# A two-layer mixer and expert block: all RWKV steps traced ahead of their outputs' norms, w_out's products between the last steps, h's rows made once, x1's affine map on VectorE

## The chip, the cores and the metric

The kernel runs on 1 core of one Trainium2 chip. A core has five engines that each work through a queue of their own in order: TensorE (PE in the profile; PEld is its loading of weights), VectorE (DVE), ScalarE (ACT), GpSimd (POOL) and SyncE (SP, which here only issues transfers). ACT and POOL issue transfers too. The metric is the device time of one execution in microseconds (us), and less is better.

## The reference, cut to what matters

Two layers over 768 tokens of 1024 numbers (256 of context, 512 of latent; the second layer keeps the latent alone after its mixer). All of it is float32.

```
p        = modulated norm of x, times w_in                     # input side
y        = [ rwkv(p) (256) | s5(p) (256) | attention(p) (512) ]
m        = (y @ w_out) * gate[s]           # s: context or latent
x1       = layer_norm(ALPHA * x + m, ln1_g, ln1_b)
h        = x1 * (1 + scale[s]) + shift[s]  # what the experts read
E, w     = two of 32 experts and their weights from h @ w_router
x2       = layer_norm(ALPHA * x1 + experts(h, E, w) * gate2[s], ln2_g, ln2_b)

rwkv:  per head a 64x64 state S, forwards and backwards over the tokens,
       S_t = S_{t-1} * w_t - (S_{t-1} kk_t) b_t^T + v_t k_t^T,   y_t = S_t r_t
       y   = (group_norm(y_f + y_b) * gn_w + gn_b + bonus) * gate(g)
```

## The kernel before, in words

The tokens lie in six tiles of 128: 0 and 1 are context, 2 to 5 latent. The kernel's functions write instructions in some order, a scheduler at build time puts them into the engines' queues by that order and by what each waits for, and the chip then runs every queue strictly in order.

**The scan.** `rwkv` runs the scan in chunks of 64 tokens: 12 steps forwards (`f`) and 12 backwards (`g`), side by side. `step(n, d)` loads the chunk's operands into `rec` (SP), corrects them by the state (L631 on PE, L633 on DVE), forms the new state (L640, L647, L653, and L656 on POOL). `output` (L672, L676 on PE, L682 on DVE) adds what this chunk yields to the tile's `y`, and is written one step late. The forward scan takes chunk 0 to 11, the backward scan 3 to 0 and then 11 to 4; so tiles 0 and 1 are complete after step 3, tiles 3 and 4 after step 9, tiles 2 and 5 after step 11.

**What follows a complete tile.** `outputs(n)` calls `finish` for a pair of tiles as soon as it is complete (the table `groups`, L721). `finish` is the group norm and the gate: DVE L695 to L714 in turn with POOL L699 to L711, then two transposes on PE (L59) and a copy to `yo`.

**mixing** is a generator that `rwkv` advances through `fill`, between its steps, so many yields a call as the third numbers of the table `FILL` say; attention and the modulation's products are advanced by the first two.

- `part(i)` multiplies the attention's and S5's 768 of the 1024 rows of `w_out` (L1582: 12 products of 128x128 by 128x512, of which the trace shows two rows each), adds ALPHA * x (L1589, L1590 on DVE), and stores the tile to `mixq`.
- `hrows(s)` makes, for context and for latent, `w2` (the first 256 rows of `w_out` times the gate, L1612 on POOL) and the two rows `hg`, `hb` of h's affine map, each spread over 128 partitions (L1615 to L1617, three POOL multiplications of 128x1024).
- `norm(i)` multiplies `yo` by `w2` (L1635 on PE), adds to `q` (the stored part), takes the statistics (L1641 to L1643 on DVE), a power on POOL (L86, L87), makes `h` by two 128x1024 operations on DVE (L1646, L1647), stores it to `hd`, and transposes it (L59; the copies to `hT` at L1656, one on DVE and one on ACT).
- `affine` makes x1 from `q`: L1659 on DVE, L1660 on ACT, L1661 and L1662 on POOL (128x1024 each), and a store that POOL issues. It is written after the next tile's norm has begun.
- `rt.logits` multiplies `hT` by the router (L1395, L1398, L1401); `rt.choose` is a chain of some 27 small DVE operations (L1423 to L1453) for two tiles, and the `rank` that it returns puts their tokens into the table of the experts' slots (PE L1458 to L1462, DVE L1464 to L1469, POOL's scatters L1473). `rt.finish` reads the table back; then tokens are gathered from `hd` (L1855), and `experts` begins with `xT` (L59 into `b_m`) and L1762.

The loop of `mixing` takes a pair of tiles through its norms once both are in `ys` and their parts are done, and otherwise makes one more part:

```python
        g = groups[0]
        if all(i in ys and i in ready for i in g):
            groups.pop(0)
            ...
            pend.insert(0, rt.choose([i - t0 for i in g]))
        else:
            if parts:
                ready.append(parts.pop(0))
                part(ready[-1])
```

`k.bank()` takes the next PSUM bank of the stream that is set; `k.free` names the streams that the last norms take instead.

After the mixer the experts' weights (3 tensors of 2 MB for each of 32 experts, from SP) stream in; the first two experts' before the first gather, the third's after it.

Of the kernel before, what the change touches and what calls it, by code (L numbers as in the profile page):

```python
# [324 lines left out]
def rwkv(k, l, st, cvd, Y, ys, streams, fill):  # L325
# [448 lines left out]
    fill('end')  # L774
# [772 lines left out]
def mixing(k, l, sO, sR, before, yd, ys, x_src, x1, hd, NTOK):  # L1547
# [8 lines left out]
    qd = k.dram('mixq%d' % l, [6, 128, D])  # L1556
    t0 = 6 - NTOK // 128
# [7 lines left out]
    gt = {}  # L1565

    def gate(s):
        if gt.get('s') != s:
            gt.update(s=s, t=brow(k, O, 'gt', mr[s, 0]))
        return gt['t']  # L1570

    def part(i):
# [13 lines left out]
        for h in range(2):  # L1586
            c = slice(512 * h, 512 * h + 512)
            o = O.tile([128, 512], F32, name='oq', bufs=2)
            V.tensor_tensor(o, ps[h], g[:, c], op=ALU.mult)  # L1589
            V.scalar_tensor_tensor(x[:, c], x[:, c], ALPHA, o, op0=ALU.mult, op1=ALU.add)  # L1590
# [3 lines left out]
    ready = []  # L1594
    for _ in range(2):
        ready.append(parts.pop(0))
        part(ready[-1])
        yield
    before()
# [7 lines left out]
    def hrows(s):  # L1607

        if rows.get('s') != s:
# [4 lines left out]
            t = P.tile([128, D], F32, name='h', bufs=2)  # L1614
# [51 lines left out]
    groups = [g for g in ((0, 1), (3, 4), (2, 5)) if g[0] >= t0]  # L1666
    pend = []

    while groups:
        g = groups[0]  # L1670
        if all(i in ys and i in ready for i in g):
            groups.pop(0)
            for j, i in enumerate(g):
                hT, late = norm(i)
                while pend:
                    pend.pop(0)()
                rt.logits(j, hT)
                (pend if groups else rt.late).append(late)
                if j == 0:
                    yield  # L1680
            pend.insert(0, rt.choose([i - t0 for i in g]))
            k.normed = not groups
            yield
        else:
            if parts:
                ready.append(parts.pop(0))
                part(ready[-1])
            while pend:
                pend.pop(0)()
            k.rest = not parts  # L1690
            yield
    while pend:
        pend.pop(0)()
# [334 lines left out]
FILL = ({'front': ((1, 0, 0), (1, 3, 0)), 'back': ((1, 3, 0),), 'inverse': ((4, 6, 0), (4, 4, 0)), 'step': ((3, 2, 0), (3, 3, 0), (2, 4, 0), (3, 3, 0), (3, 3, 0), (0, 2, 2), (0, 2, 0), (0, 0, 5))}, {'front': ((1, 0, 0), (1, 0, 0)), 'back': ((0, 0, 0), (1, 4, 0), (1, 2, 0), (1, 2, 0)), 'inverse': ((1, 9, 0),), 'step': ((2, 5, 0), (1, 4, 0), (2, 6, 0), (2, 3, 0), (1, 1, 0), (0, 0, 2), (1, 0, 0), (0, 0, 3))})  # L2028
# [56 lines left out]
def trunk(tc, a, out):  # L2085
    k = K(tc, a)
    nc = k.nc
    with ExitStack() as st:
# [50 lines left out]
        for l in range(2):  # L2139
# [45 lines left out]
            with ExitStack() as s1:  # L2185
# [4 lines left out]
                k.free = [('f', 2), ('g', 2)]  # L2190
# [79 lines left out]
```

## Time and profile before

| what | value |
|---|---|
| median of three runs | 2879.89 us (2876.12 to 2887.47) |
| the profiled execution | 2857.41 us |
| its span, first to last instruction | 2855.6 us |
| busy in the span: PE, DVE, POOL, ACT | 2201.2, 1185.0, 869.6, 524.8 us |
| TensorE clock granted, mean | 0.882 of full speed |
| moved by the transfers | 691.51 MB, 242 GB/s over the span |

The profiled execution is 22.5 us quicker than the median of the three. The stretch that the change touches is the end of each layer's scan and what lies between it and the experts: about 505 to 530 us (a place where an instruction is moved to) and 730 to 931 us in layer 0, 2130 to 2284 us in layer 1. Layer 0's experts run from 931 us, layer 1's from 2284 us.

### The profile page before, as it was taken

Reading aid. Unit: us, or ns where it says so; the run is one execution under the profiler, and the core shown is the slowest. Engines: PE = TensorE matmul, PEld = TensorE weight load, DVE = VectorE, ACT = ScalarE, POOL = GpSimd, SP = SyncE. Lnnn points to the kernel's source line nnn. Section 1 sums busy time; section 2 is a strip of 40 time slices with the busy share of each in tenths; the row PEclk is TensorE's granted clock in tenths of the full one; section 3 lists DMA queues with packets and bytes.
Section 4 is the critical chain, followed back from the end, with each engine's and each line's share of the span. In section 5 each row is a group of like instructions: output and inputs, shape, how many; then the busy total and the mean of one; then the engine's idle time right before and its main releaser. Section 6 shows DMA issues by size and latency. Waiting matters only on the chain. (4 is left out here: it accounts for less than half of the span.)

```text
span 2855.6 us, 43442 instructions
## 1 busy us (share of the span) xinstructions
PE 2201.2 (77%) x16189; PEld 1472.1 (52%) x16189; DVE 1185.0 (41%) x2830; ACT 524.8 (18%) x1264; POOL 869.6 (30%) x1189
## 2 busy tenths in 40 slices
PE   5898677878683888889874788787797397888882
PEld 3787455666442544555544676556554254454441
DVE  7972556563556000010006883666546611111114
ACT  2222333222001100011005222343120100000001
POOL 2651543331345111101105662544334510111002
PEclk8999788698886999999996899698799699999996
DMA  8334667665536899998875224556784799988994
GB/s 243 93 94 113 167 189 195 160 174 179 164 122 237 331 416 371 392 381 353 358 280 206 69 73 125 145 147 173 214 232 136 243 375 417 417 357 351 383 420 190
DMA packets 411611, 691.51 MB, mean 242 GB/s; under 512 B 146178, under 2 KB 315906, under 8 KB 394912
## 3 DMA queue, kind: packets, MB, share of 16 engines
q1 hardware_dynamic: 310368, 594.85, 58.2%
q10 hardware_dynamic: 72640, 58.03, 6.9%
q0 software_dynamic: 28288, 34.32, 3.7%
q8 instruction: 211, 3.46, 0.5%
q14 instruction: 104, 0.85, 0.1%
HBM read 607.98 MB, written 95.44 MB: 246 GB/s over the span
## 5 line engine op out<-in xcount | busy, mean ns | idle before, releaser
L1762 PE MATMUL b_m<-w,xT 128*64 128x256 f32 x4928 | 593.1, 396 | 129.3 <-DMA w<-in_expert_w_gate_dram 76.7
L1762 PEld LDWEIGHTS b_m<-w,xT 128*64 128x64 f32 x4928 | 391.6, 142 | 333.5 <-issue 150.4
L243 PE MATMUL b_m<-xT,win 128*128 128x256 f32 (+1 forms) x1416 | 276.2, 355 | 8.5 <-POOL xT L167 3.7
L243 PEld LDWEIGHTS b_m<-xT,win 128*128 128x128 f32 x1416 | 232.7, 201 | 42.9 <-POOL xT L167 4.5
L1786 PE MATMUL b_m<-w,aT 128*64 128x512 f32 x1024 | 231.0, 592 | 1.1 <-issue 0.6
L1775 DVE COPY aT<-b_m 128x256 f32<-128x256 f32 x64 | 27.2, 425 | 473.6 <-PE b_m L59 473.6
L1792 POOL DMA_INDIRECT yb<-y,dx x64 | 63.8, 997 | 427.0 <-DVEq L1907 257.3
L1786 PEld LDWEIGHTS b_m<-w,aT 128*64 128x64 f32 x1024 | 76.4, 137 | 117.1 <-issue 108.1
L1764 ACT ACTIVATE act<-b_m 128x256 f32<-128x256 f32 x64 | 24.5, 383 | 568.6 <-PE b_m L1762 556.9
L877 PE MATMUL b_a<-kz,qb 128*128 128x128 f32 (+2 forms) x416 | 113.2, 415 | 15.7 <-ACT pr L898 10.0
L1765 DVE TENSOR_TENSOR act<-act,b_m 128x256 f32<-128x256 f32 x64 | 27.0, 421 | 234.2 <-PE b_m L1762 234.2
L1582 PE MATMUL b_a<-wo,yt 128*128 128x512 f32 x240 | 111.6, 614 | 0.0
L1792 POOL DMA_INDIRECT yb<-yo,dx x13 | 12.9, 994 | 290.0 <-ACTq L1907 146.6
L877 PEld LDWEIGHTS b_a<-kz,qb 128*128 128x128 f32 x416 | 76.9, 232 | 40.5 <-ACT pr L898 11.8
L127 PE MATMUL b_a<-wmod,cc 128*32 128x128 f32 x1280 | 69.4, 329 | 35.1 <-DMA wmod<-in_w_mod_dram 29.1
L59 PE MATMUL b_a<-idf,pr 128*128 128x128 f32 x320 | 56.5, 299 | 29.6 <-DVE pt L921 11.0
L1855 POOL DMA_INDIRECT xg<-hd,ix x32 | 33.2, 1037 | 141.7 <-PE b_m L59 126.9
L1582 PEld LDWEIGHTS b_a<-wo,yt 128*128 128x128 f32 x240 | 44.9, 194 | 50.9 <-issue 49.7
L127 PEld LDWEIGHTS b_a<-wmod,cc 128*32 128x32 f32 x1280 | 40.9, 126 | 55.1 <-DMA wmod<-in_w_mod_dram 22.2
L551 POOL TENSOR_TENSOR tl<-Bm,Xh 112x4 f32<-112x4 f32 (+13 forms) x112 | 39.7, 354 | 92.5 <-DVE Xh L552 48.5
L1791 DVE TENSOR_TENSOR y<-b_m,gate 128x512 f32<-128x512 f32 x32 | 22.1, 692 | 95.0 <-PE b_m L1786 95.0
L656 POOL TENSOR_TENSOR sn<-st,gc 128x128 f32<-128x128 f32 x44 | 23.2, 529 | 121.4 <-DVE st L647 117.1
(542 smaller groups left out, 4061.5 us busy)
## 6 DMA issues: line engine op xcount, KB each, us to landing
w<-in_expert_w_gate_dram SPq DMA_DIRECT2D x64, 2048.0 KB
w<-in_expert_w_up_dram SPq DMA_DIRECT2D x64, 2048.0 KB
w<-in_expert_w_down_dram SPq DMA_DIRECT2D x64, 2048.0 KB
wmod<-in_w_mod_dram SPq DMA_DIRECT2D x80, 512.0 KB
rec<-rec SPq DMA_DIRECT2D x40, 512.0 KB
win<-in_w_in_dram SPq DMA_DIRECT2D x16, 1024.0 KB
wmod<-in_w_mod_dram SPq DMA_DIRECT2D x4, 2048.0 KB
sca<-sc SPq DMA_DIRECT2D x24, 256.0 KB
```

The costliest lines, as they stand in the source:

```text
L59: k.nc.tensor.transpose(out, x, k.idf[r:r + n, r:r + n])
L127: nc.tensor.matmul(p[32 * g:32 * g + 32, :], k.cc[:, kk, :], wt[:, kk, :], start=kk < 4, stop=kk >= 4, tile_position=(0, 32 * g))
L243: nc.tensor.matmul(p[:, :n], wt[u][:, kk, j * 128:j * 128 + 128], xT[v][:, kk, c0:c0 + n], start=kk == 0 and q == 0, stop=kk == 7 and q == 2)
L551: eng.tensor_tensor(t[:, 0:n, j:32], Bm[:, r0:r1, j:j + 1].to_broadcast([112, n, w]), x.to_broadcast([112, n, w]), op=ALU.mult)
L877: nc.tensor.matmul(dst, qb[:, 2 * v + e, :], kz[:, v, r, 128 * keys[c][0]:128 * keys[f - 1][0] + 128], start=c == 0 or (c == 4 and r == 0) ...
L1582: nc.tensor.matmul(ps[h], y[:, kt, :], wo[:, kt, 512 * h:512 * h + 512], start=kt == 0, stop=kt == 5)
L1762: mm = nc.tensor.matmul(p[64 * h:64 * h + 64, 0:256], xT[:, kk, :], w[:, kk, 256 * h:256 * h + 256], start=kk == 0, stop=kk == 7)
L1765: nc.vector.tensor_tensor(a, a, pu[:, 0:256], op=ALU.mult)
L1775: k.nc.vector.tensor_copy(aT, pa[:, 0:256].rearrange("p (j x) -> p j x", j=2))
L1786: nc.tensor.matmul(py[64 * s:64 * s + 64, :], aT[:, j, 64 * h:64 * h + 64], wd[:, q, 512 * s:512 * s + 512], start=q == 0, stop=q == 3)
L1792: sc = nc.gpsimd.indirect_dma_start(out=yb, out_offset=bass.IndirectOffsetOnAxis(ap=dst, axis=0), in_=y, in_offset=None, bounds_check=3071 ...
L1855: return nc.gpsimd.indirect_dma_start(out=out, out_offset=None, in_=hd, in_offset=bass.IndirectOffsetOnAxis(ap=idx, axis=0), bounds_check= ...
```

## The change

`finish` is called for tiles 0 and 1 after step 3 in layer 0 as before; for the pairs (3, 4) and (2, 5) it is written after all steps. `mixing` makes all parts first and then all norms in one written order, and `FILL` gives the last steps fewer yields each (2, 2, 2, 1 where each had 5 in layer 0; 1, 1, 0 where each had 3 in layer 1). `gated(s, pool)` makes `w2` from the row `gt` that `part` has loaded, and is written earlier: for context after the first two parts, for latent after the last part. `hrows()` makes both pairs of rows once, in a layout of 128 partitions by 8, with three small DVE operations, writes them to the DRAM tensor `hrow`, and each `s` then loads them spread out (ACT's queue). Both copies to `hT` are ACT's. `affine` is two 128x1024 operations on DVE. `oq` has one buffer where it had two.

```diff
-    groups = {3: (0, 1), 9: (3, 4), 11: (2, 5)}
-
     def outputs(n):
         while late:
             output(*late.pop(0))
-        if n in groups and (emit_ctx or n > 3):
-            finish(groups[n])
+        if n == 3 and emit_ctx:
+            finish((0, 1))
...
     outputs(11)
-    fill('end')
+    for g in ((3, 4), (2, 5)):
+        finish(g)
...
+    def gated(s, pool):
+        w2[s] = pool.tile([128, 2, D], F32, name='wo2%d' % s)
+        A.dma_start(w2[s], w[0:256].rearrange("(k p) n -> p k n", p=128))
+        G.tensor_tensor(w2[s], w2[s], gate(s)[:, None, :].to_broadcast([128, 2, D]), op=ALU.mult)
+
+    def hrows():
+        h, g, b = (O.tile([128, 2, 8], F32, name='h8' + n) for n in 'sgb')
+        n8 = O.tile([128, 2, 8], F32, name='h8n')
...
+        V.tensor_tensor(b, g, n8[:, 1:2].to_broadcast([128, 2, 8]), op=ALU.mult)
+        V.tensor_tensor(b, b, h, op=ALU.add)
+        V.tensor_tensor(g, g, n8[:, 0:1].to_broadcast([128, 2, 8]), op=ALU.mult)
+        A.dma_start(hr[:, 0].rearrange("s (p k) -> p s k", k=8), g)
+        A.dma_start(hr[:, 1].rearrange("s (p k) -> p s k", k=8), b)
...
     for _ in range(2):
-        ready.append(parts.pop(0))
-        part(ready[-1])
+        part(parts.pop(0))
         yield
+    if t0 == 0:
+        gated(1, O)
+    hrows()
...
-            w2 = P.tile([128, 2, D], F32, name='wo2')
-            A.dma_start(w2, w[0:256].rearrange("(k p) n -> p k n", p=128))
-            G.tensor_tensor(w2, w2, brow(k, P, 'h', mr[s, 0], bufs=2)[:, None, :].to_broadcast([128, 2, D]), op=ALU.mult)
-            hg, hb = brow(k, P, 'hg', mr[s, 2]), brow(k, P, 'hb', mr[s, 1])
-            G.tensor_tensor(t, hg, lb, op=ALU.mult)
-            G.tensor_tensor(hb, hb, t, op=ALU.add)
-            G.tensor_tensor(hg, hg, lg, op=ALU.mult)
+            rows.update(s=s, r=[brow(k, P, n, hr[s, j]) for j, n in enumerate(('hg', 'hb'))])
...
-            (A.copy if q else V.tensor_copy)(hT[:, 4 * q:4 * q + 4, :], p.rearrange("p (k t) -> p k t", k=4))
+            A.copy(hT[:, 4 * q:4 * q + 4, :], p.rearrange("p (k t) -> p k t", k=4))
 
         def affine():
-            V.tensor_scalar(sb[:, 1:2], mv[:, 0:1], sb[:, 0:1], -1.0, op0=ALU.mult, op1=ALU.mult)
-            A.activation(t, t, AF.Identity, bias=sb[:, 1:2], scale=sb[:, 0:1])
-            G.tensor_tensor(t, t, lg, op=ALU.mult)
-            G.tensor_tensor(t, t, lb, op=ALU.add)
+            V.scalar_tensor_tensor(t, t, mv[:, 0:1], lg, op0=ALU.subtract, op1=ALU.mult)
+            V.scalar_tensor_tensor(t, t, sb, lb, op0=ALU.mult, op1=ALU.add)
             G.dma_start(x1[r], t)
...
+    while parts:
+        part(parts.pop(0))
+        if not parts:
+            gated(0, P)
+            k.rest = t0 > 0
+        yield
+    late = {}
+    if t0 == 0:
+        for j in range(2):
+            hT, late[j] = norm(j)
+            rt.logits(j, hT)
+            yield
+        late[0]()
+        late[1]()
+        rank = rt.choose([0, 1])
+        k.rest = True
+        yield
+    for j, i in enumerate((3, 4)):
+        hT, late[i] = norm(i)
+        if j == 0 and t0 == 0:
+            rank()
+        rt.logits(j, hT)
+        yield
+    late[3]()
+    hT, late[2] = norm(2)
+    rank = rt.choose([3 - t0, 4 - t0])
+    rt.logits(0, hT)
+    late[4]()
+    hT, late[5] = norm(5)
+    rt.logits(1, hT)
...
-                k.free = [('f', 2), ('g', 2)]
+                k.free = 4 * [('g', 2)]
```

In the queues this moves three things that matter below. On PE at the end of layer 0's scan, before, the last forward step (its correction L631, its outputs L672) stands among the second context tile's transposes (`idf,h`), its router products (L1395) and the third part's products (L1582); the outputs' remaining products (L676) come 36 products later still:

```order
L631 MATMUL b_f<-sb_7542,rec_7798 64x128 x2
L59 MATMUL b_a<-idf,h 128x128 x8
L672 MATMUL b_f<-sb_7467,rec_7516 64x128 x2
L1395 MATMUL b_a<-hT,wr 64x128 x4
L1582 MATMUL b_a<-wo_6766,yt 128x512
L1395 MATMUL b_a<-hT,wr 64x128 x4
L1582 MATMUL b_a<-wo_6766,yt 128x512 x2
L1398 MATMUL b_a<-sel_108,r_lt 128x36
L1582 MATMUL b_a<-wo_6766,yt 128x512 x9
```

On the same queue after the change (where the parts' products are line 1602 and the norms' products of `yo` line 1644), step 9 and the corrections of step 10:

```order
L1602 MATMUL b_a<-wo_6766,yt 128x512 x16
L631 MATMUL b_f<-sb_7133,rec_7244 64x128 x2
L631 MATMUL b_g<-sb_7137,rec_7249 64x128 x2
L1602 MATMUL b_a<-wo_6766,yt 128x512 x2
L640 MATMUL b_f<-rec_7244 64x64 x4
L672 MATMUL b_f<-sb_6964,rec_7107 64x128
L640 MATMUL b_g<-rec_7249 64x64 x4
L672 MATMUL b_f<-sb_6964,rec_7107 64x128
L676 MATMUL b_f<-rec_7107 64x64 x4
L672 MATMUL b_g<-sb_6968,rec_7112 64x128 x2
L676 MATMUL b_g<-rec_7112 64x64 x4
L1602 MATMUL b_a<-wo_6766,yt 128x512 x22
```

All four parts' 48 products now stand between steps 7 and 10, and steps 10 and 11 directly follow, ahead of every transpose of `h`.

On DVE in layer 1, before, from the last tile's first operation on `h` (L1646) through the first of the two `choose` chains:

```order
L1646 SCALAR_TENSOR_TENSOR h<-q,r_mv,hg 128x1024
L1432 TENSOR_REDUCE r_m_22355<-r_e_22353 128x2
L1659 TENSOR_SCALAR r_sb<-r_mv,r_sb 128x1
L1433 TENSOR_TENSOR r_e_22353<-r_e_22353,r_m_22355 128x16
L1647 SCALAR_TENSOR_TENSOR h<-h,r_sb,hb 128x1024
L1416 SCALAR_TENSOR_TENSOR r_t_22364<-r_e_22353,rev_110 128x16
L1417 TENSOR_REDUCE r_fo_22365<-r_t_22364 128x2
L1418 TENSOR_TENSOR r_o_22362<-r_t_22364,r_fo_22365 128x16
```

and after (where L1655 and L1656 make `h`, L1668 and L1669 are the affine map on `q`, and `choose` is numbered one line lower):

```order
L1669 SCALAR_TENSOR_TENSOR q<-q,r_sb,l1b 128x1024
L1430 TENSOR_REDUCE r_e_22507<-r_sel 128x16
L1655 SCALAR_TENSOR_TENSOR h<-q,r_mv,hg 128x1024
L1431 TENSOR_REDUCE r_m_22509<-r_e_22507 128x2
L1656 SCALAR_TENSOR_TENSOR h<-h,r_sb,hb 128x1024
L1432 TENSOR_TENSOR r_e_22507<-r_e_22507,r_m_22509 128x16
L1668 SCALAR_TENSOR_TENSOR q<-q,r_mv,l1g 128x1024
L1415 SCALAR_TENSOR_TENSOR r_t_22518<-r_e_22507,rev_110 128x16
L1669 SCALAR_TENSOR_TENSOR q<-q,r_sb,l1b 128x1024
L1416 TENSOR_REDUCE r_fo_22519<-r_t_22518 128x2
L1417 TENSOR_TENSOR r_o_22516<-r_t_22518,r_fo_22519 128x16
```

L1659 is gone, and the affine operations of two tiles stand between those of the last norm and of the chain.

On POOL in layer 0, before, between the two inverses (`Xl`, `Xh` and `Bm` are theirs; `sm` is attention's):

```order
L554 COPY itm<-Xl 112x32x4
L893 TENSOR_TENSOR sm<-sink,sm 128x2
L543 MEMSET Xl 112x128
L544 MEMSET Xl 112x4
L543 MEMSET Xh 112x896
L901 TENSOR_TENSOR sm<-sm,s_5149 128x2
```

and after:

```order
L554 COPY itm<-Xl 112x32x4
L892 TENSOR_TENSOR sm<-sink,sm 128x2
L1576 TENSOR_TENSOR wo_7157<-wo_7157,gt 128x2048
L543 MEMSET Xl 112x128
L544 MEMSET Xl 112x4
L543 MEMSET Xh 112x896
L900 TENSOR_TENSOR sm<-sm,s_5149 128x2
```

The multiplication of `w2` for context, which stood some 200 us later, is now ahead of the second inverse's cleared tiles, and its 1 MB load stands on ACT's queue ahead of the first inverse's stores.

## Rows read from the trace of the kernel before

**Rows 1.** Busy time by engine in five stretches of layer 0 (header names the columns).

```profile
core 0: us, PE busy (x) PEld busy (x) DVE busy (x) ACT busy (x) POOL busy (x), PEclk, DMA share, GB/s
729.80:757.00 27.20, 22.33 (x268) 17.16 (x266) 15.04 (x41) 2.44 (x8) 3.45 (x8) 1.00 0.85 264
757.00:792.70 35.70, 15.43 (x64) 9.97 (x64) 19.05 (x33) 4.56 (x7) 27.53 (x23) 0.62 0.25 95
792.70:842.00 49.30, 44.51 (x113) 19.61 (x113) 21.37 (x45) 0.68 (x3) 17.39 (x10) 0.97 0.45 139
842.00:881.00 39.00, 27.82 (x113) 15.01 (x112) 26.66 (x45) 4.93 (x8) 27.05 (x24) 0.78 0.45 167
881.00:914.30 33.30, 7.17 (x63) 5.44 (x61) 25.20 (x77) 5.01 (x10) 17.09 (x12) 0.66 0.94 341
```

**Rows 2.** PE's timeline, layer 0: start, duration, work [idle before, its releaser].

```profile
769.11 1.97 PE L59 MATMUL b_a<-idf,h 128*128 128x128 f32 x8 [12.67 <-DVE h L1647]
...
809.23 32.84 PE L1582 MATMUL b_a<-wo,yt 128*128 128x512 f32 x72
...
846.21 0.63 PE L676 MATMUL b_f<-rec 128*64 128x64 f32 x8
...
930.76 1.97 PE L59 MATMUL b_m<-idf,xg 128*128 128x128 f32 x8 [2.51 <-DMA xg<-hd,ix]
```

**Rows 3.** DVE's timeline, layer 0: first and last of nine stretched operations, the last rank.

```profile
769.30 2.29 DVE L696 TENSOR_SCALAR gmv<-gmv 128x4 f32<-128x4 f32 x1
...
894.61 2.90 DVE L1443 TENSOR_TENSOR r_E<-r_o,r_go 128x64 f32<-128x64 f32 x1
...
914.10 0.16 DVE L1467 CAST r_pos<-r_pf 128x4 int32<-128x4 f32 x1
```

**Rows 4.** POOL's timeline, layer 0.

```profile
769.21 2.35 POOL L1661 TENSOR_TENSOR q<-q,l1g 128x1024 f32<-128x1024 f32 x1 [1.60 <-ACT q L1660]
...
785.46 1.32 POOL L86 TENSOR_SCALAR r_sb<-r_mv 128x1 f32<-128x1 f32 x1 [2.91 <-DVE r_mv L1643]
...
847.96 0.23 POOL L86 TENSOR_SCALAR r_sb<-r_mv 128x1 f32<-128x1 f32 x1
```

**Rows 5.** DVE's groups of instructions, 757 to 914.3 us: count | busy us, mean ns.

```profile
L1646 DVE SCALAR_TENSOR_TENSOR h<-q,r_mv,hg 128x1024 f32<-128x1024 f32 x6 | 7.7, 1291 | 0.1
...
L1590 DVE SCALAR_TENSOR_TENSOR xq<-xq,oq 128x512 f32<-128x512 f32 x8 | 5.5, 691 | 0.2
L1589 DVE TENSOR_TENSOR oq<-b_a,gt 128x512 f32<-128x512 f32 x8 | 5.5, 687 | 23.3 <-PE b_a L1582 23.3
...
L1656 DVE COPY hT<-b_a 128x512 f32<-128x512 f32 x6 | 4.1, 690 | 3.8 <-PE b_a L59 3.7
```

**Rows 6.** Busy time by engine in layer 1, columns as in rows 1.

```profile
2188.70:2267.50 78.80, 37.77 (x188) 21.61 (x188) 58.26 (x130) 10.68 (x20) 45.65 (x43) 0.74 0.62 218
```

**Rows 7.** PE's timeline, layer 1.

```profile
2172.10 0.65 PE L631 MATMUL b_f<-sb,rec 128*64 128x128 f32 x4
...
2177.22 0.62 PE L631 MATMUL b_f<-sb,rec 128*64 128x128 f32 x4 [0.64 <-PE b_g L676]
...
2188.05 0.63 PE L676 MATMUL b_g<-rec 128*64 128x64 f32 x8
```

**Rows 8.** DVE's timeline, layer 1: two of the seven stretched operations, the last rank.

```profile
2207.85 2.17 DVE L696 TENSOR_SCALAR gmv<-gmv 128x4 f32<-128x4 f32 x1
...
2247.54 2.91 DVE L1443 TENSOR_TENSOR r_E<-r_o,r_go 128x64 f32<-128x64 f32 x1
...
2267.30 0.16 DVE L1467 CAST r_pos<-r_pf 128x4 int32<-128x4 f32 x1
```

**Rows 9.** POOL's timeline, layer 0: the second inverse begins; `w2`'s multiplication later.

```profile
524.24 0.21 POOL L551 TENSOR_TENSOR tl<-Bm,Xh 112x4 f32<-112x4 f32 x1 [8.32 <-DVE Bm L541]
...
794.79 4.53 POOL L1612 TENSOR_TENSOR wo<-wo,h 128x2048 f32<-128x2048 f32 x1
```

**Rows 10.** Busy time by engine in layer 0's experts, columns as in rows 1.

```profile
1000.00:1200.00 200.00, 166.98 (x1172) 97.11 (x1170) 16.42 (x35) 17.43 (x35) 22.86 (x23) 0.95 0.96 392
```

More of the change, by code (lines that the diff above doesn't have):

```diff
@@ L1556, in mixing @@
     qd = k.dram('mixq%d' % l, [6, 128, D])
+    hr = k.dram('hrow%d' % l, [2, 2, 1024])
     t0 = 6 - NTOK // 128
@@ L1564, in mixing @@
         xg, xb = brow(k, O, 'xg', a['ln2_g'][0]), brow(k, O, 'xb', a['ln2_b'][0])
-    gt = {}
+    gt, w2 = {}, {}
     def gate(s):
@@ L1587, in part @@
             c = slice(512 * h, 512 * h + 512)
-            o = O.tile([128, 512], F32, name='oq', bufs=2)
+            o = O.tile([128, 512], F32, name='oq')
             V.tensor_tensor(o, ps[h], g[:, c], op=ALU.mult)
@@ L1605, in mixing @@
     rows = {}
-    def hrows(s):
-        if rows.get('s') != s:
-            w2 = P.tile([128, 2, D], F32, name='wo2')
-            A.dma_start(w2, w[0:256].rearrange("(k p) n -> p k n", p=128))
-            G.tensor_tensor(w2, w2, brow(k, P, 'h', mr[s, 0], bufs=2)[:, None, :].to_broadcast([128, 2, D]), op=ALU.mult)
-            hg, hb = brow(k, P, 'hg', mr[s, 2]), brow(k, P, 'hb', mr[s, 1])
-            t = P.tile([128, D], F32, name='h', bufs=2)
-            G.tensor_tensor(t, hg, lb, op=ALU.mult)
-            G.tensor_tensor(hb, hb, t, op=ALU.add)
-            G.tensor_tensor(hg, hg, lg, op=ALU.mult)
-            rows.update(s=s, r=(w2, hg, hb))
-        return rows['r']
     def norm(i):
         s = 1 if i < 2 else 0
-        w2, hg, hb = hrows(s)
+        if rows.get('s') != s:
+            rows.update(s=s, r=[brow(k, P, n, hr[s, j]) for j, n in enumerate(('hg', 'hb'))])
+        hg, hb = rows['r']
         t = R.tile([128, D], F32, name='q', bufs=3)
@@ L1634, in norm @@
             for kt in range(2):
-                nc.tensor.matmul(ps[h], y[:, kt, :], w2[:, kt, 512 * h:512 * h + 512], start=kt == 0, stop=kt == 1)
+                nc.tensor.matmul(ps[h], y[:, kt, :], w2[s][:, kt, 512 * h:512 * h + 512], start=kt == 0, stop=kt == 1)
         st = rt.new('st', [128, 2, 6])
         mv = rt.new('mv', [128, 2], bufs=3)
-        sb = rt.new('sb', [128, 2], bufs=3)
+        sb = rt.new('sb', [128, 1], bufs=3)
         for h in range(2):
@@ L1643, in norm @@
         V.bn_aggr(mv, st)
-        rsqrt(k, sb[:, 0:1], mv[:, 1:2], 1e-5)
+        rsqrt(k, sb, mv[:, 1:2], 1e-5)
         h = P.tile([128, D], F32, name='h', bufs=2)
         V.scalar_tensor_tensor(h, t, mv[:, 0:1], hg, op0=ALU.subtract, op1=ALU.mult)
-        V.scalar_tensor_tensor(h, h, sb[:, 0:1], hb, op0=ALU.mult, op1=ALU.add)
+        V.scalar_tensor_tensor(h, h, sb, hb, op0=ALU.mult, op1=ALU.add)
         r = slice(128 * (i - t0), 128 * (i - t0) + 128)
-        k.store = (A if groups else nc.sync).dma_start(hd[r], h)
+        k.store = (nc.sync if i in (2, 5) else A).dma_start(hd[r], h)
         hv = h.rearrange("t (p k) -> t k p", k=8)
@@ L1662, in affine @@
-            G.tensor_tensor(t, t, lb, op=ALU.add)
+            V.scalar_tensor_tensor(t, t, mv[:, 0:1], lg, op0=ALU.subtract, op1=ALU.mult)
+            V.scalar_tensor_tensor(t, t, sb, lb, op0=ALU.mult, op1=ALU.add)
             G.dma_start(x1[r], t)
         return hT, affine
[L1666 to L1682, printed above, removed]
-            yield
[L1684 to L1691, printed above, removed]
@@ L1692, in mixing @@
-    while pend:
-        pend.pop(0)()
+    while parts:
[9 more added lines that the diff above has]
+            rt.logits(j, hT)
+            yield
+        late[0]()
[9 more added lines that the diff above has]
+        yield
@@ L1694, in mixing @@
+    late[3]()
[5 more added lines that the diff above has]
+    rt.logits(1, hT)
+    k.normed = True
+    yield
+    rank()
+    rt.choose([2 - t0, 5 - t0])()
+    rt.late = [late[2], late[5]]
     rt.finish()
@@ L2023, in combine @@
             put(None, None, None, None)
-FILL = ({'front': ((1, 0, 0), (1, 3, 0)), 'back': ((1, 3, 0),), 'inverse': ((4, 6, 0), (4, 4, 0)), 'step': ((3, 2, 0), (3, 3, 0), (2, 4, 0), (3, 3, 0), (3, 3, 0), (0, 2, 2), (0, 2, 0), (0, 0, 5))}, {'front': ((1, 0, 0), (1, 0, 0)), 'back': ((0, 0, 0), (1, 4, 0), (1, 2, 0), (1, 2, 0)), 'inverse': ((1, 9, 0),), 'step': ((2, 5, 0), (1, 4, 0), (2, 6, 0), (2, 3, 0), (1, 1, 0), (0, 0, 2), (1, 0, 0), (0, 0, 3))})
+FILL = ({'front': ((1, 0, 0), (1, 3, 0)), 'back': ((1, 3, 0),), 'inverse': ((4, 6, 0), (4, 4, 0)), 'step': ((3, 2, 0), (3, 3, 0), (2, 4, 0), (3, 3, 0), (3, 3, 0), (0, 2, 2), (0, 2, 0), (0, 0, 2), (0, 0, 2), (0, 0, 2), (0, 0, 1))}, {'front': ((1, 0, 0), (1, 0, 0)), 'back': ((0, 0, 0), (1, 4, 0), (1, 2, 0), (1, 2, 0)), 'inverse': ((1, 9, 0),), 'step': ((2, 5, 0), (1, 4, 0), (2, 6, 0), (2, 3, 0), (1, 1, 0), (0, 0, 2), (1, 0, 0), (0, 0, 1), (0, 0, 1), (0, 0, 0))})
 TILES = ({'z': (0,), 't': (0, 0, 0, 0, 0, 1, 0, 1), 'e': (1, 1, 1, 2, 1, 2, 2, 1), 'r': (0, 1, 0, 1, 0, 1, 0, 2), 'o': (0, 0)}, {'z': (1,), 't': (0, 0, 0, 0, 0, 0, 0, 0), 'e': (1, 1, 1, 1, 2, 1, 1, 1), 'r': (0, 1, 0, 1, 0, 1, 0, 1), 'o': (0, 0)})
```

5 lines of the change are left out of this document (4 added, 1 removed).

## The prediction

> **What bounds the kernel now.** I read the busy times by stretch first, for which engine is full where; then PE's timeline, for the order in which the scan's end and the parts lie and what ends its idle time; then DVE's and POOL's timelines side by side. The reader should see three things.
>
> First, the experts wait for one event. They are fed by transfers at 392 GB/s with the transfer engines 96% busy, PE 167 of 200 us [rows 10], and they begin when the first gathered tokens are transposed, at 930.76 us [rows 2], 16.7 us after the second pair's last rank on DVE at 914.10 [rows 3]. In layer 1 that rank is at 2267.30 [rows 8]. The third expert's weights are requested after the first gather, so whatever brings the rank forward brings all that follows forward, as long as the first two experts' weights are there. What the change is worth is therefore how far these two ranks move.
>
> Second, before the rank in layer 0 the engines take turns instead of overlapping. From 757 to 792.7 us PE is busy 15.4 of 35.7 us (it first waits 12.67 us for context's `h`) while POOL is busy 27.5 [rows 1, 2]; from 792.7 to 842 PE is busy 44.5 of 49.3 with the parts while DVE is busy 21.4 [rows 1]; the last forward step's outputs end only at 846.8 [rows 2], so `finish` for tiles 2 and 5, and all behind it, comes later still. From 842 to 914.3 PE is busy 35 of 72 us and DVE 52 [rows 1].
>
> Third, DVE is busy with waiting there: nine small operations last 1.7 to 2.9 us, where their like take 0.2 to 0.4. The first is L696, 2.29 us from 769.30 [rows 3], which ends with POOL's L1661 from 769.21 for 2.35 us [rows 4]; the last is L1443 with 2.90 [rows 3]. Their excess adds to 17.9 us in layer 0. In layer 1 seven such after 2188.7, from L696 to L1443 [rows 8], hold 12.4 us.
>
> **The scan's end and the parts, layer 0.** PE's order sets when the last step ends. From 729.8 us it now has: 22.3 us of steps and context products that already lay before 757 [rows 1], the last forward step's rest (L631, L672, L676), some 2.9 us by the like of L676's 0.63 for eight [rows 2], and four parts, 96 products at 32.84/72 = 0.456 us [rows 2], 43.8 us. That is 69.0 us, so 798.8 without idle time. Between steps 10 and 11 little else stands, and the steps' own handoffs to DVE left PE idle 4.9 of 27.2 us before [rows 1]; I charge half, and take 801 us as the end of the scan and of the parts. Before, they ended at 847: 46 us earlier, paid by the 12.67 and what else PE idled in 757 to 792.7, with context's norms no longer in front.
>
> **DVE's work after it, layer 0.** From 757 to 914.3 DVE is busy 19.05 + 21.37 + 26.66 + 25.20 = 92.3 us [rows 1]. From that go 17.9 of excess (POOL keeps only `finish`'s small multiplications and the power; the three of L1615 to L1617 and the two of each affine are gone), 11.0 for the parts' L1589 and L1590 [rows 5], which now lie under the steps, 4.1 for copies to `hT` [rows 5], which ACT takes (idle nearly all along [rows 1]), and 1.3 for L1659. Added are two affine operations for six tiles, priced as L1646, the same operation on the same shape, 1.29 us [rows 5]: 15.4. That makes 73.4. Norm 0's share, 7.9 us, lies before the last step's end by the queue; 1.0 of `finish` that lay before 757 comes back. So 67 us of DVE follow 801.
>
> How densely DVE works through them is the main unknown. Before, it was busy 68% of 842 to 881 and 76% of 881 to 914 [rows 1], and 58.26 of 78.80 us, 74%, in layer 1 [rows 6], where POOL's long multiplications, and norms and `finish` written one pair after another, made it wait. Now four tiles' `finish` and then their norms stand together, and affine operations lie in the gaps, but `finish` and the power still go to POOL and back. Bounds: 100% gives a rank at 868, 68% at 899.5. I take 82%, about midway: 801 + 81.7 = 883, **31 us earlier** (15 to 46).
>
> **Layer 1.** Step 9 took from 2172.10 to 2177.22 [rows 7], after the last part; it now lies before the last nine of that part's products. Its 5.1 us of elapsed time become some 3.2 of PE work in front of them, so the steps end near 2187 instead of 2188.7 [rows 7], and the last forward chunk comes with them. DVE after it: 58.26 [rows 6], less 12.4 of excess, 2.8 for `hT`, 0.9 for L1659, 1.7 of scan, plus 8 x 1.29 = 10.3 for the affine map and 3.9 of `finish` that came before 2188.7: 54.7, say 55. At 82% it takes 67 us, and the rank comes at 2254, **13 us earlier** (at 68% 0, at 100% 25).
>
> **What else moves.** `w2`'s multiplication for context, 4.53 us [rows 9], goes ahead of the second inverse on POOL. POOL idled 8.32 us before that inverse's first product at 524.24 [rows 9], which covers it if its 1 MB and the row `gt` have landed by some 519 us; cost 0, and up to 5 us if the load, ahead of the first inverse's stores on ACT's queue, holds them up. `hrows` runs under the parts; its reload for latent waits on ACT's queue for norm 1's `h`, with two transfers behind it; DVE has `finish` to do meanwhile, so 0, with 2 to 3 us if that cover is gone. `oq` with one buffer makes a product's DVE pair wait for itself, which is in order anyway: 0. The tail's rsqrt on POOL can be held by DVE's affine operations: L86 takes 0.23 us alone and 1.32 beside L1646 [rows 4]. In ten norms that is up to 11 us if each is hit once more. I count it in the density, not on top.
>
> The sum is 31 + 13 = **44 us**: 2857.4 becomes about 2813 for the profiled execution. The median of the runs is 22.5 us above that execution, and I carry the difference over: **2836 us**.
>
> The Trainium skill, "SBUF — State Buffer", section "Who interferes with whom", says that DVE and GpSimd share one pair of ports under an exclusive lock: a DVE operation with two SBUF inputs and a GpSimd operation that reads SBUF don't overlap, and whichever starts second waits to the other's end. The trace agrees in both directions, with L696's 2.29 us and L86's 0.23 against 1.32 [rows 3, 4]. By that rule the change takes long holds of the pair from POOL and gives DVE twenty new ones (the affine operations, two SBUF inputs each) of up to 1.3 us; if every one shut out a POOL operation that DVE then waits for, the sum would be 22 us instead of 44.
>
> **The rivals.**
> - *Handoffs to POOL lengthen.* Each norm's power, and the seven or so POOL operations of each `finish`, find DVE in an affine operation; DVE then waits for POOL. Worth 1.1 us at each of ten norms and at about as many places in the two `finish` groups, 22 us: rank gains of about 22 us in all instead of 44, 2858. For it: 1.32 against 0.23 [rows 4]. Against: most affine operations stand behind the last `finish`. The page named above states this lock in general.
> - *The experts do not start earlier.* If the first two experts' weights, or ACT's queue with its added loads, hold the gather where it was, nothing is won: 2880. Against: before, the second expert's weights follow tile 5's store by SP, so they move with it, and the transfer engines are 45% busy from 792.7 to 881 [rows 1].
> - *DVE alone is already the bound, and gets more work.* Then the tails lengthen by what DVE gains: 15.4 + 10.3 less 4.1, 2.8, 1.3 and 0.9, that is 16.6 us: 2896. It decides if the tails have no DVE idle time for it and the excess does not go; against it, DVE idles 65 of 157 us from 757 to 914 [rows 1], and PE's end of the scan, not DVE, holds the last `finish`.
>
> **How the numbers follow.** My forecast, both ranks 20 to 65 us earlier together, has 0.62, and its own range is 2815 to 2860. Handoffs have 0.22 (about 2850 to 2872), no earlier start 0.10, DVE as the bound 0.06. The range leaves out the last and half of the one before: 2808 to 2872. About 0.5%, 14 us, is what a measurement of this kernel can tell from no change. Faster by more: 0.62 and three quarters of the handoffs, 0.78; within it 0.16; slower 0.06.
>
> **What would show it.** Right: PE without the 12.67 us gap, the parts' products between steps 7 and 10, the last L676 near 801; no small DVE operation above 1.5 us in choose; the last L1467 near 883 in layer 0, and 13 us earlier than layer 0's shift alone in layer 1; the first transposed tokens 16 to 17 us after the rank. Wrong: a rank after 900 with DVE idle on POOL's L87 or L711; a gather that waits for SP or ACT; more than 8 us of POOL idle time at the second inverse.

## The result, and the profile after

The changed kernel takes 2847.5 us (median of four runs, 2838.1 to 2856.2) against 2879.8 for the kernel before in the same comparison: a ratio of 0.990 (95% interval 0.987 to 0.993). That is 32 us less; 44 were forecast, and 2836 us. The profiled execution spans 2847.1 us.

First the busy times by engine, for the three stretches that the prediction divides layer 0's end into. They are to be held against [rows 1].

```profile
core 0: us, PE busy (x) PEld busy (x) DVE busy (x) ACT busy (x) POOL busy (x), PEclk, DMA share, GB/s
757.00:801.00 44.00, 41.55 (x232) 23.46 (x232) 23.37 (x43) 0.90 (x2) 4.05 (x6) 1.00 0.42 154
801.00:842.00 41.00, 25.96 (x117) 14.27 (x113) 33.96 (x82) 4.74 (x13) 24.00 (x30) 0.79 0.46 168
842.00:884.30 42.30, 18.27 (x106) 12.05 (x102) 30.72 (x95) 5.09 (x14) 17.56 (x18) 0.67 0.72 256
```

PE is busy 41.55 of the 44 us in which the steps and parts now stand together, where it was busy 15.4 of 35.7. DVE then does 64.7 us of work in 83.3 (78%). PE's timeline of the changed kernel (L1602 is a product of a part) shows where this leads:

```profile
766.15 19.15 PE L1602 MATMUL b_a<-wo,yt 128*128 128x512 f32 x44
...
795.87 0.63 PE L676 MATMUL b_g<-rec 128*64 128x64 f32 x8
...
908.18 1.97 PE L59 MATMUL b_m<-idf,xg 128*128 128x128 f32 x8 [2.36 <-DMA xg<-hd,ix]
910.08 2.40 PE L1776 MATMUL b_m<-w,xT 128*64 128x256 f32 x10
```

The last step's product comes at 795.87, 50 us earlier than in [rows 2], and the gap of 12.67 us is gone. The first gathered tokens are transposed at 908.18 where they were at 930.76. So layer 0's experts begin 22.6 us earlier. DVE's timeline shows the last rank (now L1466), and a wait ahead of it that was not forecast; ACT's, what stands behind that wait:

```profile
863.08 0.69 DVE L1650 TENSOR_TENSOR q<-b_g,q 128x512 f32<-128x512 f32 x1 [7.06 <-DMA q<-mixq]
...
884.27 0.16 DVE L1466 CAST r_pos<-r_pf 128x4 int32<-128x4 f32 x1
```

```profile
858.54 0.33 ACTq L1635 DMA_DIRECT2D q<-mixq  x1
858.92 0.21 ACT L1424 ACTIVATE r_ge<-r_gd 128x8 f32<-128x8 f32 x1 [8.25 <-DMA x<-q]
```

The rank is at 884.27; the forecast was 883. The wait is norm 5's: `q` has three buffers, the fourth latent tile's load (L1635) must wait until x1 of the first has been stored from its buffer, and DVE, in order, waits 7.06 us for the load.

The rank is 29.8 us earlier than in [rows 3], the experts only 22.6: between the two, 7.2 us are lost. POOL's last scatter of the ranks and its first gather, and SP's queue, show it:

```profile
889.03 1.68 POOL L1472 DMA_INDIRECT tab<-tokd,r_pos  x1 [0.31 <-issue]
903.93 1.05 POOL L1869 DMA_INDIRECT xg<-hd,ix  x1 [13.22 <-DVE r_li L1535]
```

```profile
855.98 17.72 SPq L1658 DMA_DIRECT2D hd<-h  x2
873.80 0.37 SPq L1838 DMA_DIRECT2D w<-in_expert_w_gate_dram  x1
874.27 0.73 SPq L1838 DMA_DIRECT2D w<-in_expert_w_up_dram  x1
875.09 0.44 SPq L1838 DMA_DIRECT2D w<-in_expert_w_down_dram  x1
899.76 0.34 SPq L1502 DMA_DIRECT2D r_ti<-tab  x1
```

The table of slots is read (L1502) 10.7 us after the last scatter was issued. Before, these two were 3.1 us apart, by SP's and POOL's timelines of the kernel before:

```profile
890.41 0.37 SPq L1824 DMA_DIRECT2D w<-in_expert_w_gate_dram  x1
...
922.03 0.34 SPq L1503 DMA_DIRECT2D r_ti<-tab  x1
```

```profile
918.90 1.68 POOL L1473 DMA_INDIRECT tab<-tokd,r_pos  x1 [0.30 <-issue]
```

What changed is how far ahead of the rank the second expert's 6 MB are requested: 23.7 us before (890.41 to 914.10), 10.5 us now (873.80 to 884.27). The windows of the changed kernel show the transfer engines full from 880 to 890 us and still 82% busy in the 10 us behind, though they move less than half as much there (152 GB/s), and the other engines do next to nothing:

```profile
880.00:890.00 10.00, 0.32 (x5) 0.21 (x5) 8.92 (x43) 0.20 (x1) 7.41 (x8) 0.50 1.08 377
890.00:900.00 10.00, 0.00 (x0) 0.00 (x0) 0.00 (x0) 0.00 (x0) 0.71 (x1) 0.50 0.82 152
```

The transfer engines fall quiet only from 899 to 900 us (13% busy), and the read follows at 899.76. In the kernel before they were 1% busy from 914 to 922 us, while the last four scatters went out.

Layer 1 repeats both, in DVE's and SP's timelines: a wait for `q`, the rank, and a table read 27.8 us after the weights were requested, 11.8 after the last scatter (2254.35).

```profile
2224.45 0.69 DVE L1650 TENSOR_TENSOR q<-b_g,q 128x512 f32<-128x512 f32 x1 [5.31 <-DMA q<-mixq]
...
2249.57 0.16 DVE L1466 CAST r_pos<-r_pf 128x4 int32<-128x4 f32 x1
```

```profile
2238.40 0.39 SPq L1838 DMA_DIRECT2D w<-in_expert_w_gate_dram  x1
...
2266.16 0.34 SPq L1502 DMA_DIRECT2D r_ti<-tab  x1
```

### The profile page after: what moved, and what is told of

It reads as the page before. It is cut to its first block, busy times and chain, and to the rows that moved or that the text cites. A ratio compares the mean times of both kernels' runs of the same rounds, so it can differ in the third digit from the quotient of the medians.

```text
span 2847.1 us, 43425 instructions
## 1 busy us (share of the span) xinstructions
PE 2222.6 (78%) x16189; PEld 1485.8 (52%) x16189; DVE 1165.4 (41%) x2836; ACT 517.5 (18%) x1264; POOL 805.1 (28%) x1160
## 5 line engine op out<-in xcount | busy, mean ns | idle before, releaser
L1789 DVE COPY aT<-b_m 128x256 f32<-128x256 f32 x64 | 27.2, 425 | 475.2 <-PE b_m L59 475.2
L1602 PE MATMUL b_a<-wo,yt 128*128 128x512 f32 x240 | 112.7, 614 | 0.0
L876 PEld LDWEIGHTS b_a<-kz,qb 128*128 128x128 f32 x416 | 79.0, 237 | 43.5 <-ACT pr L897 15.4
L1602 PEld LDWEIGHTS b_a<-wo,yt 128*128 128x128 f32 x240 | 44.0, 193 | 47.4 <-issue 46.0
L503 PE MATMUL b_g<-ar,bz 128*128 128x128 f32 (+1 forms) x384 | 61.0, 322 | 3.8 <-ACT bz L495 3.8
```

The source lines that it names most:

```text
L503: nc.tensor.matmul(pv[:, cp, q, 0:n, :], bk[:, hp, q, cp].rearrange("p s t -> p (s t)"), ar[:, 0:n, cp, q, :], start=True, stop=True)
L876: nc.tensor.matmul(dst, qb[:, 2 * v + e, :], kz[:, v, r, 128 * keys[c][0]:128 * keys[f - 1][0] + 128], start=c == 0 or (c == 4 and r == 0) ...
L1602: nc.tensor.matmul(ps[h], y[:, kt, :], wo[:, kt, 512 * h:512 * h + 512], start=kt == 0, stop=kt == 5)
L1789: k.nc.vector.tensor_copy(aT, pa[:, 0:256].rearrange("p (j x) -> p j x", j=2))
```

## The experiments

**Theory and rivals.** The theory: the new order brings the rank forward as forecast, and two transfer waits take part of it back, one for `q` (too few buffers) and one for the table behind the second expert's weights. Rivals: the table's delay belongs to the scatters or to the queue that reads, not to the weights; the affine map's move to DVE, not the order, makes the gain; and the odd layer 1, where the unchanged input side seemed to lose 14 us, is an effect of the change.

**The kernel itself, again** (`after_again`, no edit). 

> The changed kernel once more, unaltered. In the first profile of it the last ranks came 29.8 and 17.7 us earlier by the clock of the span, but the experts only 22.4 and 8.8 us; and layer 1's input side, whose instructions did not change, lost 15 us of the lead. Theory A (that loss is chance: the granted TensorE clock falls differently from execution to execution): the ratio to the kernel before stays near 0.989, and in this profile layer 1's rank shift is not bound to repeat the loss; layer 0's rank again near 884 us and the first expert near 910. Theory B (the change itself slows layer 1's input side): the lead again falls from about 22 to about 8 us between 1760 and 2060 us.

It took 2841.4 us, ratio 0.988 (0.985 to 0.991). Both waits were there again: 6.28 and 6.21 us for `q`, and a table read 24 and 28 us after the weights.

**A fourth buffer for `q`** (`q4`).

```diff
-        t = R.tile([128, D], F32, name='q', bufs=3)
+        t = R.tile([128, D], F32, name='q', bufs=4)
...
-        t2 = self.P.tile([16, 2, NB * 64, 2], I32, name='f_t2', tag='q', bufs=3)
+        t2 = self.P.tile([16, 2, NB * 64, 2], I32, name='f_t2', tag='q', bufs=4)
```

> The changed kernel with four buffers instead of three for the stored part q (and the table that shares them). Theory A (DVE's 7.06 us wait for the last norm's q in layer 0, and 5.31 us in layer 1, is a wait for a buffer that the x1 store of an earlier norm still reads, and it lies on the path): both waits go, the last rank comes 5 to 7 us earlier in layer 0 and 4 to 5 in layer 1, and if the weights of the second expert move along with the last h store, the time falls by 8 to 12 us, 0.3 to 0.4%. Rival B (the table's reading waits for the second expert's weights whatever the rank does): ranks earlier by as much, but the first expert's start and the time unchanged within 3 us.

2835.8 us, ratio 0.9855 (0.982 to 0.989), with the kernel as changed beside it at 0.988. The two intervals overlap, so the 6 us between the medians are not clear of the noise; the trace is. No wait for `q` is left, and the ranks come at 878.94 and 2233.6. But the weights' request moves along with the tiles, and the table is again read 26.5 us after it, by SP's timeline of this run:

```profile
867.87 0.39 SPq L1838 DMA_DIRECT2D w<-in_expert_w_gate_dram  x1
...
894.40 0.34 SPq L1502 DMA_DIRECT2D r_ti<-tab  x1
```

So the rank to first expert still takes 25.7 us. This speaks for the weights: the read keeps its distance to them, not to the scatters.

**The second expert's weights right behind the first's** (`early_w1`).

```diff
                 wts.get(0)
+                wts.get(1)
...
-                with tc.issue_after(k.store.ins):
-                    wts.get(1)
```

> The changed kernel with the second expert's weights requested right behind the first's, ahead of the last two h stores in SP's queue, instead of after the last h store. Theory A (the 9 us between the last scatter and the table's reading, 1.5 before the change, are transfers queued with these 6 MB): the weights lie at about 834 to 866 us in layer 0, the table is read 1.5 to 3 us after the last scatter, and the first expert starts 6 to 8 us earlier in each layer: time down 12 to 16 us, 0.4 to 0.6%. Rival B (the scatters themselves, or POOL, are late for another reason): the distance from scatter to reading stays at 9 us and the time within 3 us. A cost on either: the q load for the last norm shares the engines with the weights and may lengthen the 7 us wait.

2851.6 us, ratio 0.990 (0.986 to 0.994), and a median 10 us above the changed kernel's, where 12 to 16 less were expected; the runs of the two overlap (2838.6 to 2863.4, and 2834.0 to 2851.9), so that it is slower is not shown, only that nothing is won. The table is read 2.6 us after the last scatter (903.40 to 906.04), with the transfer engines 2% busy while the scatters go out, so the weights were its delay. But now the same 6 MB stand ahead of x1's store and `q`'s load. DVE's timeline of this run:

```profile
876.88 0.69 DVE L1650 TENSOR_TENSOR q<-b_g,q 128x512 f32<-128x512 f32 x1 [18.21 <-DMA q<-mixq]
...
898.63 0.16 DVE L1466 CAST r_pos<-r_pf 128x4 int32<-128x4 f32 x1
```

The wait of 7.06 us has become 18.21, and the rank is 14.4 us later.

**Both** (`q4_early_w1`, the two diffs above). 

> Both edits together. If both waits are what held the gain back (theory A of each), the time falls by the sum, 18 to 28 us below the changed kernel, near 2822 us, and the first expert of layer 0 starts near 896 us. Rival: the two waits overlap, or the weights' traffic lengthens the q loads, and the sum is no more than the better one of the two.

2820.7 us, ratio 0.981 (0.978 to 0.984), 21 us under the changed kernel on the same chip. No wait for `q`, and SP's read, POOL's last scatter and PE's first expert stand close together:

```profile
882.21 0.34 SPq L1502 DMA_DIRECT2D r_ti<-tab  x1
```

```profile
879.34 0.96 POOL L1472 DMA_INDIRECT tab<-tokd,r_pos  x1 [0.30 <-issue]
```

```profile
894.05 12.67 PE L1776 MATMUL b_m<-w,xT 128*64 128x256 f32 x96
```

From rank (874.57) to first expert is 19.5 us, close to the 18.6 of before.

**The second expert's weights behind the gather** (`late_w1`).

```diff
-                with tc.issue_after(k.store.ins):
-                    wts.get(1)
                 *_, rt = mixes
                 gs = gathers(k, rt, wts, hd, NTOK, *rows)
+                wts.get(1)
```

> The changed kernel, with the second expert's weights requested behind the first gather instead of behind the last tile's store of h. The work is the same. If the 6 MB in flight are what holds up the table's scatters and its read, the read follows the last scatter by about 3 us instead of 9 to 12 in both layers, and the first expert's first product follows the last rank by about 18 to 19 us instead of 26, while the wait of norm 5 for q stays near 7 us, since those weights were requested after it. The experts then lack weights that were on their way: 6 MB at 400 GB/s are 15 us, of which the first expert's own products hide some, so the time should be 2845 to 2865, no better than the changed kernel. If the delay of the table's read has another cause (the scatters themselves, or the queue of the engine that reads), it stays at 9 us or more, and the first expert at 26 us behind the rank.

2848.7 us, ratio 0.991 (0.988 to 0.994). The edit did not do what was meant: none of the three tensors is requested behind the gather. The first stands right behind the table's read (894.54 us, 4.7 ahead of the first gather's issue), and the scheduler put the other two ahead of tile stores (828.95 and 850.48). That still takes the weights away from the scatters: the table is read 2.4 and 3.2 us after the last scatter, with the transfer engines 2% busy while the scatters go out, and the first expert follows the rank by 19.0 and 20.8 us, as the theory had it. The wait for `q`, though, is not 7 but 14.99 us, since 2 MB more were requested ahead of x1's store; that takes most of this back, and the time is no better, by DVE's timeline:

```profile
865.10 0.69 DVE L1650 TENSOR_TENSOR q<-b_g,q 128x512 f32<-128x512 f32 x1 [14.99 <-DMA q<-mixq]
```

**The order alone** (`order_only`): the changed order, with the affine map on DVE's small operation, ACT and POOL, and the first copy to `hT` on DVE, as before.

```diff
...
-            V.scalar_tensor_tensor(t, t, mv[:, 0:1], lg, op0=ALU.subtract, op1=ALU.mult)
-            V.scalar_tensor_tensor(t, t, sb, lb, op0=ALU.mult, op1=ALU.add)
+            V.tensor_scalar(sb2, mv[:, 0:1], sb, -1.0, op0=ALU.mult, op1=ALU.mult)
+            A.activation(t, t, AF.Identity, bias=sb2, scale=sb)
+            G.tensor_tensor(t, t, lg, op=ALU.mult)
+            G.tensor_tensor(t, t, lb, op=ALU.add)
```

> The changed kernel's order (all steps ahead of the norms, parts between the last steps, w2 and h's rows made early) with the old engines for two things: x1's affine map on DVE, ACT and POOL as before, and the first copy to hT on DVE. Theory A (the order brings the gain: the end of the scan and of the parts moves from 847 to about 801 us; where the affine map runs is worth little, since its operations take DVE as long as the operations that POOL's stretch): last L682 near 802 us in layer 0, small DVE operations of 2 us and more beside POOL's multiplications again, 8 to 14 us of them in layer 0; time within 8 us of the changed kernel's, ratio to before 0.986 to 0.992. Rival B (the affine map on DVE, which lets the choice chain run undisturbed, brings most of it): ratio 0.995 to 1.0.

2849.4 us, ratio 0.990 (0.9875 to 0.993): about all of the gain. Its rank in layer 0 is at 896.63, 12 us later than with the map on DVE, and the stretched DVE operations are back, as DVE's and POOL's timelines of this run show side by side:

```profile
866.07 3.24 DVE L1657 SCALAR_TENSOR_TENSOR h<-h,r_sb,hb 128x1024 f32<-128x1024 f32 x1
...
874.54 2.29 DVE L1417 TENSOR_TENSOR r_go<-r_t,r_fo 128x8 f32<-128x8 f32 x1
```

```profile
865.89 2.33 POOL L1671 TENSOR_TENSOR q<-q,l1g 128x1024 f32<-128x1024 f32 x1
868.30 3.22 POOL L1672 TENSOR_TENSOR q<-q,l1b 128x1024 f32<-128x1024 f32 x1
...
874.43 2.36 POOL L1672 TENSOR_TENSOR q<-q,l1b 128x1024 f32<-128x1024 f32 x1
```

DVE's L1657 begins just behind POOL's L1671 and takes 3.24 us, where its like in the changed kernel (L1656) takes 1.28 at most norms and 1.75 at the longest; DVE's small L1417 begins 0.11 us behind POOL's L1672 and ends with it. The Trainium skill, "SBUF — State Buffer", section "Who interferes with whom", gives this lock between the two engines; the traces here agree. (L1657 and L1417 each read two tensors in SBUF. The prediction's example L696 reads one, and was held all the same, for 2.29 us.)

What the exchange of engines is worth can be read from the start of the scan's last product (the last L676) to the rank. In layer 0 that takes 93.8 us here and 81.6 in `q4`, in layer 1 73.1 and 67.0; none of these waits for `q`. So the exchange is worth 12 and 6 us at the two ranks. In the changed kernel, 88.0 and 73.3 us, the wait for `q` takes 6 us of it back in each layer. What is left is 5.8 us in layer 0 and nothing in layer 1. Layer 0's first expert comes 13.5 us later here (923.6 against 910.1); most of the rest is the scan, whose last product stands 6.5 us later, and why is not shown. The ratios, with intervals of some 8 us to either side, do not part the two kernels.

**The engines alone** (`engines_only`): the order before, with the affine map on DVE and both copies to `hT` on ACT (the reverse of that exchange, put into the kernel before). 

> The kernel before, in its old order and with its old rows of h and w2, with only x1's affine map on DVE and both copies to hT on ACT. Theory A (small by itself: the nine and seven stretched operations lose most of their 17.9 and 12.4 us, DVE gets 14 and 9 us of new operations, and the rank's path keeps PE's late end of the scan): 0 to 12 us faster, ratio 0.996 to 1.0, the scan of layer 0 still ending at 847 us less what context's norms gain, first expert at 920 to 931 us. Rival B (the engine change alone carries the gain): ratio 0.988 to 0.992. Rival C (DVE as the bound gets 16 us more to do): ratio 1.003 to 1.006.

2870.5 us, ratio 0.997 (0.995 to 0.999), a small gain. The rank in layer 0 is at 919.67, no earlier than before, and the first expert at 940.14, where 920 to 931 was expected. In layer 1 the rank comes 74.1 us after the scan's last product starts, 4.7 less than before. So in the old order the same exchange of engines moves neither rank by anything like the forecast.

This run also bears on the table's delay. The second expert's weights are requested 17.6 and 18.1 us ahead of the rank, between the 24 of before and the 10 to 15 of the changed order, and the read follows the last scatter by 4.2 and 6.4 us, between the 3 to 4 of before and the 8 to 12 of the changed order.

**The kernel before, again** (`before_again`, no edit). 

> The kernel before, unaltered, one more profiled execution. Its first profiled execution took 2857.4 us, 18 to 22 us less than the median of its runs. Theory A (layer 1's input side got a higher granted clock there by chance; the changed kernel does not slow it): in this execution the same instructions from 1760 to 2100 us take 5 to 15 us longer than in the first profile, and the whole some 2870 to 2880 us. Rival B (the changed kernel slows that stretch): the stretch takes as long as in the first profile, within 2 us.

Span 2879.2 us, 23.6 longer than the first profiled execution of the same kernel. The table shows where, in us, from the timelines of PE and DVE (the scan's start is the first L631 of layer 1; its last product is the last L676, taken at its start):

| run | rank, layer 0 | to first expert | last expert to layer 1's scan | that to its rank | of it, from the scan's last product | rank to first expert |
|---|---|---|---|---|---|---|
| before | 914.1 | 18.6 | 547.0 | 233.3 | 78.8 | 18.8 |
| before, again | 917.6 | 18.3 | 560.6 | 236.3 | 78.8 | 19.5 |
| changed | 884.3 | 25.8 | 560.1 | 224.0 | 73.3 | 27.0 |
| changed, again | 884.0 | 23.3 | 548.6 | 233.8 | 74.2 | 27.2 |
| `q4` | 878.9 | 25.7 | 553.9 | 220.0 | 67.0 | 26.3 |
| `early_w1` | 898.6 | 19.3 | 554.5 | 236.8 | 80.0 | 21.9 |
| `q4_early_w1` | 874.6 | 19.5 | 553.0 | 215.7 | 67.1 | 21.3 |
| `late_w1` | 886.9 | 19.0 | 553.1 | 230.1 | 77.2 | 20.8 |
| `order_only` | 896.6 | 27.0 | 556.0 | 221.7 | 73.1 | 23.4 |
| `engines_only` | 919.7 | 20.5 | 550.8 | 230.4 | 74.1 | 24.2 |

The time up to layer 1's scan is work that the change doesn't touch; in two executions of one kernel it differs by 13.6 us before and 11.5 after. So the changed kernel's seeming loss there is chance. The longer executions are those with the lower granted clock, 0.80 and 0.79 of full speed in this stretch against 0.82 and 0.81, and DVE's busy time in it is the same within 1 us (344.0 to 344.8). The scan itself varies in the same way: in the changed kernel 150.8 and 159.7 us from its first product to the start of its last, at 0.94 and 0.89. The stretch from there to the rank varies by 1 us at most in two executions of one kernel, so the work behind the scan is to be read from its last product.

## Why the prediction was right, and where its sizes were off

- **The scan's end and the parts** (801 us, 46 earlier): right, and a little better. The last product stood at 795.87. PE was busy all of 729.8 to 792.7, so the idle time that was charged did not come.
- **DVE's work after it** (67 us at 82%): 64.7 us of work at 78%. The rank at 884.27 against 883, 31 us forecast and 29.8 found. The density was the main unknown and held, but not for the reason given: 7.06 us of its idle time are the wait for `q`'s buffer, which no step of the prediction names. Without it (`q4`) the rank is 5.3 us earlier. That the rank fell within 1.3 us of the forecast is therefore in part luck: an earlier scan's end and less work made up for a wait that was not in the sum.
- **The excess of small operations**: gone, as forecast: none in `choose` takes more than 0.74 us. The longest DVE operations left in the tail, of 128x1024, take 1.75. The order alone brings excess back (`order_only`).
- **"The second expert's weights follow tile 5's store by SP, so they move with it"**: this is the step that was mis-sized, and with it the 16.7 us from the rank to the gathered tokens, which became 23.9 (884.27 to 908.18). The weights moved 16.6 us (890.41 to 873.80), the rank 29.8, since part of what the change removes from DVE stands between that store and the rank. The table is read 24 to 28 us after the weights' request, in both layers of two executions of the changed kernel and of one of `q4`, however early the rank is. The rival "the experts do not start earlier" holds for about 7 us of each layer, not for the whole; `early_w1`, `late_w1` and `q4_early_w1` show its cause by bringing the distance back to 19 to 22 us.
- **Layer 1** (13 us): the work was priced right, and the time was not got. From the scan's last product to the rank, 67 us were forecast and 78.8 measured before; `q4` takes 67.0 and `q4_early_w1` 67.1 (in `q4` by 52.5 us of work at 79%, where 55 at 82% were summed, so two small misses cancel). The changed kernel takes 73.3 and 74.2, and the wait for `q` (5.31 and 6.21 us) is all but 1 us of the difference. The scan ahead of it takes 155.2 us by the mean of two executions and 156.0 before, with a spread of 9, so the 1.7 us forecast there cannot be seen. The rank is thus some 5 us earlier, and the 8 us more between rank and experts (27.1 against 19.1) take that back. Layer 1 wins nothing.
- **The sum**: layer 0's experts begin 25.6 us earlier by the means of two executions each (908.7 against 934.2), and layer 1 adds nothing, where 44 were forecast. The spans of these four executions differ by 23.9 us by the same means, about what the two layers give. The medians give 32 and 34 us; the 8 to 10 more belong to executions without a trace, and are not placed. The 22.5 us that the prediction carried from the profiled execution to the median were that one execution's own: the second profile of that kernel took 2881.0 us, the first of the changed one 2848.9 against a median of 2847.5.
- **`gated` ahead of the second inverse** (0, unless POOL idles over 8 us there): the sign that was to show it wrong did come. POOL sat idle 12.87 us before that inverse's first product, by POOL's timeline, which now begins 7.3 us later than in [rows 9]:

```profile
531.50 0.21 POOL L551 TENSOR_TENSOR tl<-Bm,Xh 112x4 f32<-112x4 f32 x1 [12.87 <-DMA rec<-xa]
```

The wait is for a load of `xa`, which fits the step's upper bound (stores on ACT's queue held up by the added load), though no run here took that load away. It cost nothing that lasted: the last L631 before the changed stretch starts at 729.2 us against 728.2 before.
- **One buffer for `oq`, and the rows' reload** (0): right. L1609 waits 22.0 us for PE's products where L1589 waited 23.3 before, and DVE waits for no reloaded row.
- **The rivals**: handoffs to POOL are a small part of the tail, by DVE's waits in the changed kernel from 801 to 885 us (us in total, times, longest). Four groups wait for POOL and make 7.1 us (a wait of L700 for POOL's L699, 0.3 us, is the fourth), where that rival asked for 11 more in each layer. In layer 0's tail of the kernel before, from 757 us on, such waits made 22.1 us; in layer 1's they made 8.7, and 8.6 now. POOL's power is still held, as that rival said (L86 takes 0.70 to 1.65 us at five of six norms, 0.23 at the sixth), but DVE has other work meanwhile and waits 1.1 us for it in all. Nor did DVE become the bound: the tails did not lengthen by the work that it gained.

```profile
DVE q L1650 <- DMA q<-mixq: 7.1, 1, 7.1
DVE y L706 <- POOL gvv L703: 3.2, 2, 1.8
DVE y L714 <- POOL y L711: 2.8, 3, 1.3
...
DVE h L1656 <- POOL r_sb L87: 0.8, 2, 0.4
```

## What to carry to other kernels

Moving an event forward is worth what the next thing behind it allows: list the bulk transfers that were requested shortly before it and check that each moves as far as the event does, because small scatters and reads that follow may be held up until those bytes are through, as the table's read was here: 24 to 28 us after 6 MB were requested, however early the rank came. Count buffers when work that was spread out is written one behind another: the fourth of four tiles waits for the first one's store. And where two waits trade the same bytes, remove both together: here one edit alone gave 6 us and the other lost 10, neither clear of the noise, and both together gave 21, which is.

## What the runs showed of the hardware

- The small scatters that POOL issues were held by 6 MB that SP had requested: from the issue of the last scatter to the table's read it took 8 to 12 us with these bytes in flight (the changed kernel, `q4` and `order_only`), 2.4 to 4.3 without (before, `early_w1`, `late_w1`, `q4_early_w1`). The Trainium skill, "DMA: Bandwidth & Descriptors", section "Issuing engines are not separate DMA queues", says that transfers issued by different engines share the same transfer engines and interleave; the trace agrees, with 10.7 us against 3.1.
- The 6 MB were slow there too: from 889 to 895 us of the changed kernel the transfer engines were 98% busy and moved 70 GB/s, where they moved 403 from 880 to 882. Why is not shown.
- The load of one tile of `q`, with the store before it, cost DVE in layer 0 7.06, 14.99 and 18.21 us with 6 MB of weights requested ahead of it, with 2 MB more ahead of it and 2 MB during the store, and with 12 MB (changed, `late_w1`, `early_w1`).
- The same instructions of layer 1's input side took 547.0 and 560.6 us in two executions of one kernel, at a granted clock of 0.82 and 0.80.
